# Grouped-query attention on one core: another order of the first query and key work, and a last unit whose final key chunk is closed apart

## The chip, the cores and the metric

The kernel runs on one NeuronCore of a Trainium2 chip. The core has five engines that work side by side, each through its own list of instructions in order: TensorE (PE) multiplies matrices, ScalarE (ACT) applies functions such as exp, VectorE (DVE) and GpSimd (POOL) do elementwise work, and SyncE (SP) issues transfers. ACT and POOL issue transfers too. Operands lie in the on-chip memory SBUF, and PE writes its results to PSUM, from where ACT and DVE read them. Engines wait for each other by semaphores.

The metric is the device time of one execution in microseconds (us). Less is better.

## The reference

```python
batch, seq, n_heads, n_kv_heads, dim = 8, 512, 32, 8, 64      # Q, K, V in float32
scale = 1.0 / np.sqrt(dim)
K_expanded = np.repeat(K, heads_per_group, axis=2)            # 4 query heads per key head
V_expanded = np.repeat(V, heads_per_group, axis=2)
scores = np.einsum('bhqd,bhkd->bhqk', Q, K_expanded) * scale  # after transposes to b, h, s, d
weights = np.exp(scores - np.max(scores, axis=-1, keepdims=True))
weights = weights / (np.sum(weights, axis=-1, keepdims=True) + 1e-10)
output = np.einsum('bhqk,bhkd->bhqd', weights, V_expanded)
return output.transpose(0, 2, 1, 3).astype(np.float32)
```

## The kernel before

**Units and tiles.** The work is cut into 32 units: 8 batches times 4 pairs of key heads. A unit has 8 query heads, two key heads, 512 queries and 512 keys. It is computed as 4 head pairs with 4 key chunks of 128 each, which makes 16 score tiles, numbered 0 to 15 within the unit (tile t belongs to head pair t // 4 and key chunk t % 4). `mm_scores` (L261) makes one tile: two matmuls with 64 contraction rows, one for each head of the pair, give 128 keys x (2 heads x 512 queries) in one of three PSUM slots. The scores come out transposed, keys on the partitions, so that the exponentials can be the weights of the next matmul.

**Exponentials.** A tile's exp is made by ACT (`exp_act`, L276, into tiles called `pa`) or by DVE (`exp_dve`, L285). The list `TILES` says which: 0 is ACT, 1 is DVE with one multiply and add whose result is read as bf16 bits (`pd`), 2 is DVE likewise (`lo`) followed by two additions on POOL (`hi`, L302, and `sum`, L308) that average two such approximations. Of 16 tiles, 11 are ACT's and 5 are DVE's; in all units the tile of kind 2 is tile 7. No maximum is subtracted.

**Outputs.** `mm_out` (L312) makes one output block: 128 queries of one head, four matmuls over the key chunks with the exponentials as weights, against the 64 value columns and a column of ones (65 in all, so that the sum of weights comes out beside the output). Blocks are grouped; a group fills one of two PSUM buffers called `x`, which the transposes use too. `take_out` (L328) copies a group to SBUF (`raw`), and after the unit's end `divide` (L352) takes the reciprocal on DVE (L355) and multiplies, on POOL (L360, two instructions of 128 x 1024 per unit), into `o_sb`, which `store` (L369) sends out by SP's queue. In the last unit the groups have 4 blocks (16 matmuls) each, eight groups in all; its first 16 blocks are multiplied by POOL, the next 8 by DVE (L360, 128 x 512), and the last two groups are multiplied by DVE straight from PSUM (128 x 256 each). The store of the very last group is issued on SP ahead of those of the unit's first 16 and next 8 blocks, that of the last but one on ACT's queue.

**Transposes.** Queries and keys are loaded with a cast to bf16 by POOL's queue (`load_q`, `load_k`, `load_v`; the first load of queries, `q_nat`, holds heads 4 to 7 of unit 0) and transposed on PE (`mm_turn`, L377), with a copy by DVE (`take_turn`, L389). Keys need a second copy with the two heads swapped, which two transfers on SP make (L395, L396). `spread_v` copies values beside the ones on POOL.

**The order.** Everything is recorded in an order planned ahead: the class `Plan` (L20) walks through the tiles with assumed costs, hands score tiles to ACT and DVE in the pattern `SCORES`, fills PE's time between them with transposes and output blocks, and returns one list of operations. The main loop (L494) records them in that order; nothing is moved afterwards, and each engine runs its list strictly in order. The planner's costs were not changed by the edit.

**The start.** Unit 0 does not wait for the casting loads. The first key pair (`k32`, 256 KB) and the first four query heads (`q32`, two halves of 256 KB) come in float32 by SP's and ACT's queues. DVE casts the keys (L468) and makes the swapped copy (L469, L470), ACT casts the first query half (L471). `turn_first` (L475) transposes, four transposes a time: keys, queries, swapped keys. Ten matmuls on zeros (L466) run on PE before that. The second query half is cast by DVE (L484) ahead of the main loop, and transposed in the main loop after the second score tile.

Of the kernel before, what the change touches and what calls it, by code (L numbers as in the profile page):

```python
# [11 lines left out]
BF16 = mybir.dt.bfloat16  # L12
# [8 lines left out]
NEVER = 1e9  # L21


class Plan:
# [14 lines left out]
    def __init__(self, nu, tiles, scores, fill, groups, arrive, x_cost, x_behind, fix, nslot, nx, npt):  # L39
        self.ops = []  # L40
        qa = [16 * u + t for u in range(nu) for t in range(16) if not tiles[t]]
        qd = [16 * u + t for u in range(nu) for t in range(16) if tiles[t]]
# [10 lines left out]
        def run_dve(until):  # L53
            nonlocal behind
            while ready:
# [9 lines left out]
                if j[1] == "score":  # L65
                    cost, vis = self.SCH, self.SCH_VIS
                    slots[j[3]] = start + vis
                    pt[j[2]] = start + vis + (fix if tiles[j[2] % 16] == 2 else 0.0)
# [102 lines left out]
def kernel(  # L171
# [24 lines left out]
    TILES = [int(c) for c in "0100010201000100"]  # L196
    SCORES = "AADAADAADAADAADA"
# [78 lines left out]
    def exp_act(t):  # L276
        pts[t] = pa_pool.tile([128, 2, S], BF16, name="pa")
        nc.scalar.activation(  # L278
            out=pts[t],
            in_=score.pop(t),  # L280
            func=mybir.ActivationFunctionType.Exp,
            scale=float(scale),
        )

    def exp_dve(t):  # L285
        two = TILES[t % len(TILES)] == 2
# [25 lines left out]
    def mm_out(f, at):  # L312
        _, u, lo, n = f
        if at == 0:
            xs[f] = xpsum.tile([128, 2048], U8, name="x").bitcast(FP32)
        i, r = divmod(lo + at, BLK)
        m, qc = divmod(r, SC)
        for kc in range(SC):
# [86 lines left out]

    turned = {}
# [26 lines left out]
    def arrive(f):  # L433
# [3 lines left out]
        NU, TILES, SCORES, FILL, groups, arrive, x_cost, x_behind,  # L437
# [3 lines left out]
    with tc.manual_schedule(engines={PE, ACT, DVE, POOL, SP}):  # L441
# [4 lines left out]
        k16 = first.tile([128, SC, 2, 2 * D], BF16, name="k16")  # L446
        warm = first.tile([128, S], BF16, name="warm")
        nc.sync.dma_start(out=k32, in_=rows(K, 0, 0, 2))
        nc.scalar.dma_start(out=q32[:, :, 0:2 * D], in_=rows(Q, 0, 0, 2))
        nc.sync.dma_start(out=q32[:, :, 2 * D:4 * D], in_=rows(Q, 0, 2, 4))  # L450
# [11 lines left out]
        load_q(1)  # L462

        xw = xpsum.tile([128, 2048], U8, name="x").bitcast(FP32)
        for _ in range(10):
            nc.tensor.matmul(xw, warm[:, 0:128], warm, start=True, stop=True)  # L466

        nc.vector.tensor_copy(out=k16[:, :, 0, :], in_=k32)  # L468
        nc.vector.tensor_copy(out=k16[:, :, 1, 0:D], in_=k32[:, :, D:2 * D])  # L469
        nc.vector.tensor_copy(out=k16[:, :, 1, D:2 * D], in_=k32[:, :, 0:D])  # L470
        nc.scalar.copy(out=q16[:, :, 0:2 * D], in_=q32[:, :, 0:2 * D])  # L471
# [3 lines left out]
        def turn_first(src, copy, dst):  # L475
            x = xpsum.tile([128, 2048], U8, name="x").bitcast(BF16)
            for sc in range(SC):
                nc.tensor.transpose(x[:, sc * 128:(sc + 1) * 128], src[:, sc, :], ident)  # L478
            copy(out=dst, in_=x[:, 0:S])  # L479
# [73 lines left out]
```

## Time and profile before

| | us |
|---|---|
| Median of 3 runs | 357.85 (357.47 to 357.93) |
| The profiled execution | 357.47 |
| Its span | 355.5 |
| Around the span | 1.97 |
| PE busy | 341.1 |
| DVE busy | 336.3 |
| ACT busy | 334.0 |
| POOL busy | 280.8 |
| First exp of ACT starts | 7.79 |
| Last exp of ACT starts | 343.92 |
| Last multiply of DVE starts | 349.46 |

All rows but the first two are of one profiled execution, in microseconds from the start of its span. Busy time counts an instruction from start to end, and instructions of one engine overlap at their ends: an exp is shown with 1.02 us, while the next one on ACT can start 0.90 after it. A row of a timeline gives start, duration, engine, source line, operation, output and input, and in brackets how long the engine was idle before and what released it. Rows of POOL are rough. A row of the table of stages gives, for a stretch, the busy time and number of instructions of PE, PE's weight loads, DVE, ACT and POOL, the clock that TensorE was granted (1.00 is full), the share of the transfer engines and GB/s.

### The profile page before, as it was taken

To read this page: it belongs to the slowest core of one execution; us is meant where nothing else is said; L and a number is where in the kernel's file an instruction comes from. 1 tells how busy PE (TensorE), PEld (TensorE's weight loads), DVE (VectorE), ACT (ScalarE), POOL (GpSimd) and SP (SyncE) were. 2 spreads that over 40 slices of the span, in tenths; PEclk is the share of its full clock that TensorE was granted. 3 is DMA by queue.
4 is the path that set the end of the run, shared out by engine and by line. 5 is a ranking of instruction groups with operands and counts; after the bars stand their busy time and mean duration, and the time that the engine had idled before them with its cause. 6 is when DMAs were issued, how large, how long until landed. Compare 5 with 4: busy or idle time off the path is not lost.

```text
span 355.5 us, 13278 instructions
## 1 busy us (share of the span) xinstructions
PE 341.1 (96%) x5774; PEld 223.9 (63%) x5774; DVE 336.3 (95%) x462; ACT 334.0 (94%) x355; POOL 280.8 (79%) x200
## 2 busy tenths in 40 slices
PE   7899999999999999999999999999999999999980
PEld 3366666666666666666666666666666666666660
DVE  3799999999999999999999999999999999999883
ACT  4999999999999999999999999999999999999960
POOL 6287977989778997789788897798977898866691
PEclk9899999999999999999999999999999999999997
DMA  8989765898778976699667987689757996722346
GB/s 181 207 146 193 194 162 157 190 208 204 171 181 190 258 191 143 128 236 240 164 182 168 205 209 193 157 189 246 192 129 181 202 251 177 190 75 79 120 164 194
DMA packets 51481, 64.42 MB, mean 181 GB/s; under 512 B 3424, under 2 KB 36064, under 8 KB 51424
## 3 DMA queue, kind: packets, MB, share of 16 engines
q0 software_dynamic: 25344, 24.91, 46.3%
q1 hardware_dynamic: 25024, 38.28, 31.7%
q8 instruction: 45, 0.74, 0.8%
q10 hardware_dynamic: 1056, 0.39, 0.4%
q14 instruction: 12, 0.10, 0.1%
HBM read 50.86 MB, written 33.55 MB: 237 GB/s over the span
## 4 chain that ended last, share of the span: by engine, by line
ACT 60%; issue 24%; PE 11%; DVE 3%; ACTq 0%; DVEq 0%
ACT pa L278 60%; PE x L319 4%; DVE pd L292 2%; PE x L466 1%; PE x L387 1%; DVE qt L401 0%; PE x L478 0%; DVE kt L479 0%; DVE raw L339 0%; PE s_256 L267 0%; PE s_237 L267 0%; ACTq L278 0%; DVE inv L355 0%; PE s_261 L267 0%; DVE o_sb L360 0%
## 5 line engine op out<-in xcount | busy, mean ns | idle before, releaser
L360 POOL TENSOR_TENSOR o_sb<-raw,inv 128x1024 f32<-128x1024 f32 x63 | 118.4, 1896 | 45.9 <-DVE inv L355 45.9
L319 PEld LDWEIGHTS <-pa 128*128 128x128 bf16 x2816 | 135.2, 98 | 29.4 <-issue 29.1
L319 PEld LDWEIGHTS <-pd 128*128 128x128 bf16 x1024 | 100.1, 98 | 0.6 <-issue 0.5
L267 PEld LDWEIGHTS <-kt 64*128 64x128 bf16 x1024 | 53.7, 94 | 71.6 <-issue 45.5
L339 DVE COPY raw<-x 128x455 f32<-128x455 f32 (+3 forms) x161 | 89.0, 570 | 0.7 <-PE x L319 0.5
L308 POOL TENSOR_TENSOR sum<-lo,hi 128x1024 bf16<-128x1024 bf16 x32 | 68.1, 2127 | 2.5
L302 POOL TENSOR_TENSOR hi<-lo,shift 128x512 int32<-128x512 int32 x32 | 40.8, 1275 | 9.3 <-DVE lo L292 9.2
L387 PE MATMUL x<-ident,q_nat 128*128 128x128 bf16 x504 | 44.3, 220 | 0.2 <-DMA q_nat<-in_Q_dram 0.2
L401 DVE COPY qt<-x 128x1024 bf16<-128x1024 bf16 x63 | 42.9, 681 | 0.0
L387 PEld LDWEIGHTS <-q_nat 128*128 128x128 bf16 x504 | 29.5, 97 | 16.0 <-issue 15.5
L237 POOL DMA_DIRECT2D q_nat<-in_Q_dram x32 | 25.6, 799 | 0.0
L319 PEld LDWEIGHTS <-sum 128*128 128x128 bf16 x256 | 24.8, 97 | 0.0
L319 PE MATMUL x<-v_5039,pa 128*128 128x65 bf16 x352 | 19.5, 194 | 0.0
L319 PE MATMUL x<-v_6090,pa 128*128 128x65 bf16 x352 | 19.4, 194 | 0.0
L319 PE MATMUL x<-v_2937,pa 128*128 128x65 bf16 x352 | 19.4, 194 | 0.0
L319 PE MATMUL x<-v_3988,pa 128*128 128x65 bf16 x352 | 19.4, 194 | 0.0
L319 PE MATMUL x<-v_835,pa 128*128 128x65 bf16 x352 | 19.4, 194 | 0.0
L319 PE MATMUL x<-v_1886,pa 128*128 128x65 bf16 x352 | 19.4, 194 | 0.0
L319 PE MATMUL x<-v_7141,pa 128*128 128x65 bf16 x352 | 19.0, 194 | 0.4 <-DVE raw L339 0.4
L319 PE MATMUL x<-v_5039,pd 128*128 128x65 bf16 x128 | 17.4, 194 | 0.0
L319 PE MATMUL x<-v_6090,pd 128*128 128x65 bf16 x128 | 17.3, 194 | 0.0
L319 PE MATMUL x<-v_2937,pd 128*128 128x65 bf16 x128 | 17.3, 194 | 0.0
(1091 smaller groups left out, 994.0 us busy)
## 6 DMA issues: line engine op xcount, KB each, us to landing
out_dram<-o_sb SPq DMA_DIRECT2D x30, 1024.0 KB, 4.8
q_nat<-in_Q_dram POOLq DMA_DIRECT2D x31, 512.0 KB, 5.9
k_nat<-in_K_dram POOLq DMA_DIRECT2D x8, 512.0 KB, 8.4
v_nat<-in_V_dram POOLq DMA_DIRECT2D x8, 512.0 KB, 11.0
kt<-kt SPq DMA_DIRECT2D x62, 64.0 KB, 5.3
out_dram<-o_sb SPq DMA_DIRECT2D x3, 512.0 KB, 3.6
q_105<-in_Q_dram ACTq DMA_DIRECT2D x1, 256.0 KB, 4.4
k_106<-in_K_dram SPq DMA_DIRECT2D x1, 256.0 KB, 3.9
```

Source lines behind the costliest of these rows:

```text
L237: nc.gpsimd.dma_start(out=t[:, :, lo * D:], in_=rows(Q, b, HU * gp + lo, HU * (gp + 1)))
L267: nc.tensor.matmul(s[:, m, :], kt[u][64 * m:64 * m + 64, 0 if m == g else 1, kc * 128:(kc + 1) * 128], qt[u][64 * m:64 * m + 64, i, :], st ...
L278: nc.scalar.activation(out=pts[t], in_=score.pop(t), func=mybir.ActivationFunctionType.Exp, scale=float(scale),)
L292: nc.vector.tensor_scalar(out=bits, in0=score.pop(t), scalar1=float(A_schr), scalar2=float(B_two if two else B_one), op0=mybir.AluOpType.mult,
L302: nc.gpsimd.tensor_tensor(out=high.rearrange("p m s -> p (m s)").bitcast(I32), in0=bits.rearrange("p m s -> p (m s)").bitcast(I32), in1=shift,
L308: nc.gpsimd.tensor_tensor(out=dst, in0=bits.bitcast(BF16), in1=high.bitcast(BF16), op=mybir.AluOpType.add)
L319: nc.tensor.matmul(xs[f][:, at * D1:(at + 1) * D1], pts[(u * HPG + i) * SC + kc][:, m, qc * 128:(qc + 1) * 128], v1[u][:, kc, 2 * i // HPG ...
L339: nc.vector.tensor_copy(out=raws[u][:, lo:lo + n, :], in_=x[:, 0:n * D1])
L360: eng.tensor_tensor(out=osbs[u].rearrange("p qc h d -> p h qc d")[:, lo // SC + h0:lo // SC + h0 + nh], in0=src[:, :, 0:D].rearrange("p (h ...
L387: nc.tensor.transpose(xs[f][:, at * 128:(at + 1) * 128], src, ident)
L401: nc.vector.tensor_copy(out=qt[u][:, 2 * part:2 * part + 2, :], in_=x)
L466: nc.tensor.matmul(xw, warm[:, 0:128], warm, start=True, stop=True)
```

## The change

The diff touches the first tiles and the last unit. Between them every engine has the same instructions in the same order.

*At the start.* The first key load is split: 128 keys (64 KB) first, the other 384 after the first query half has been issued. The first 128 keys are cast and swapped by DVE, transposed (both copies, two transposes) and copied in one go. The first query half is cast and copied by DVE instead of ACT. The other 384 keys are cast by ACT, swapped by POOL, transposed after the first score tile (six transposes) and copied by DVE in one instruction of 768 columns. The second query half is cast, transposed and copied after the fourth score tile: DVE's list has its cast behind DVE's first exp, where the cast was ahead of the main loop before. `load_v(0)` is issued ahead of POOL's swaps and of the cast of the first values, where it was behind that cast. There are 8 matmuls on zeros instead of 10.

*In the last unit.* The tile of kind 2 is tile 3 instead of 7. The exp of the very last tile is made in two halves, one per head. The last two output groups do their first three key chunks for all eight blocks, and then the fourth chunk for each group. The planner, which gets the tile kinds, puts the unit's last six score tiles ahead of all its output groups; before, the first head pair's outputs stood between them.

```diff
+    LAST_TILES = [int(c) for c in "0102010001000100"]
...
     def exp_act(t):
         pts[t] = pa_pool.tile([128, 2, S], BF16, name="pa")
+        dst, src = pts[t], score.pop(t)
+        for ms in (slice(0, 1), slice(1, 2)) if t == 16 * NU - 1 else (slice(0, 2),):
+            nc.scalar.activation(out=dst[:, ms, :], in_=src[:, ms, :],
...
-    def mm_out(f, at):
+    def mm_out(f, at, kcs=tuple(range(SC))):
         _, u, lo, n = f
-        if at == 0:
+        if at == 0 and kcs[0] == 0:
             xs[f] = xpsum.tile([128, 2048], U8, name="x").bitcast(FP32)
...
-        for kc in range(SC):
+        for kc in kcs:
...
+    def tile_kind(t):
+        return (LAST_TILES if t >= 16 * (NU - 1) else TILES)[t % 16]
...
-        nc.sync.dma_start(out=k32, in_=rows(K, 0, 0, 2))
+        nc.sync.dma_start(out=k32[:, 0:1], in_=rows(K, 0, 0, 2)[:, 0:1])
         nc.scalar.dma_start(out=q32[:, :, 0:2 * D], in_=rows(Q, 0, 0, 2))
+        nc.sync.dma_start(out=k32[:, 1:SC], in_=rows(K, 0, 0, 2)[:, 1:SC])
         nc.sync.dma_start(out=q32[:, :, 2 * D:4 * D], in_=rows(Q, 0, 2, 4))
         nc.sync.dma_start(out=v32, in_=rows(V, 0, 0, 2))
...
         load_q(0, lo=HPG)
         load_k(0)
         load_q(1)
+        load_v(0)
...
-        for _ in range(10):
+        for _ in range(8):
             nc.tensor.matmul(xw, warm[:, 0:128], warm, start=True, stop=True)
...
+        def cast_k(lo, hi, natural, swapped):
+            natural(out=k16[:, 0, lo:hi, :], in_=k32[:, lo:hi, :])
+            swapped(out=k16[:, 1, lo:hi, 0:D], in_=k32[:, lo:hi, D:2 * D])
+            swapped(out=k16[:, 1, lo:hi, D:2 * D], in_=k32[:, lo:hi, 0:D])
+
+        def turn_k(lo, hi):
+            x = xpsum.tile([128, 2048], U8, name="x").bitcast(BF16)
+            n = hi - lo
+            for c in range(2):
+                for sc in range(lo, hi):
+                    j = c * n + sc - lo
+                    nc.tensor.transpose(x[:, j * 128:(j + 1) * 128], k16[:, c, sc, :], ident)
+            nc.vector.tensor_copy(
+                out=kt[0][:, :, lo * 128:hi * 128],
+                in_=x[:, 0:2 * n * 128].rearrange("p (c s) -> p c s", c=2),
+            )
+
+        def turn_q(i):
+            lo, hi = 2 * i * D, 2 * (i + 1) * D
+            nc.vector.tensor_copy(out=q16[:, :, lo:hi], in_=q32[:, :, lo:hi])
+            x = xpsum.tile([128, 2048], U8, name="x").bitcast(BF16)
             for sc in range(SC):
+                nc.tensor.transpose(x[:, sc * 128:(sc + 1) * 128], q16[:, sc, lo:hi], ident)
+            nc.vector.tensor_copy(out=qt[0][:, i, :], in_=x[:, 0:S])
+
+        cast_k(0, 1, nc.vector.tensor_copy, nc.vector.tensor_copy)
+        turn_k(0, 1)
+        turn_q(0)
+        cast_k(1, SC, nc.scalar.copy, nc.gpsimd.tensor_copy)
         nc.gpsimd.tensor_copy(
             out=v1f[:, :, :, 0:D], in_=v32.rearrange("p sc (h d) -> p sc h d", h=2)
         )
-        load_v(0)
         load_q(2)
         load_q(3)
...
+        ends = [(NU - 1, 3 * BLK), (NU - 1, 3 * BLK + 4)]
...
+            elif kind == "out" and (what[0] if engine == "pe" else what)[1:3] in ends:
+                continue
...
+                if what[0] > 0 and scored < 100:
+                    turn_k(1, SC)
+                    scored = 100
                 mm_scores(*what)
+                scored += 1
+                if scored == 103:
+                    turn_q(1)
                     spread_v(0)
...
+        final = [("out", u, lo, 4) for u, lo in ends]
+        for kcs in (tuple(range(SC - 1)), (SC - 1,)):
+            for f in final:
+                for at in range(4):
+                    mm_out(f, at, kcs)
+                if kcs[-1] == SC - 1:
+                    take_out(f, NEVER)
```

## The prediction

> **What bounds the kernel now.** I read the page's busy shares first, then the table of stages, then the timelines of the first 24 and the last 15 us, because the diff leaves everything between them in the same order on every engine.
>
> ```profile
> span 355.5 us, 13278 instructions
> ...
> PE 341.1 (96%) x5774; PEld 223.9 (63%) x5774; DVE 336.3 (95%) x462; ACT 334.0 (94%) x355; POOL 280.8 (79%) x200
> ```
>
> ```profile
> 30.00:40.00 10.00, 9.95 (x175) 6.57 (x171) 9.99 (x14) 9.88 (x12) 8.26 (x7) 1.00 0.88 209
> ```
>
> The reader is to see that PE, DVE and ACT are all full between 20 and 330 us (the second fence is one row of the table of stages: busy time of PE, PEld, DVE, ACT and POOL in a stretch of 10). They feed each other in fixed orders. A stream that enters that stretch later leaves it later by as much; a saving counts only at the two ends.
>
> The start, from the timelines of DVE, ACT and PE (start, duration, engine, line):
>
> ```profile
> 6.88 0.43 DVE L479 COPY kt<-x 128x512 bf16<-128x512 bf16 x1 [0.47 <-PE x L478]
> 7.22 0.55 DVE L484 CAST q_108<-q_105 128x512 bf16<-128x512 f32 x1
> 8.33 0.42 DVE L479 COPY qt<-x 128x512 bf16<-128x512 bf16 x1 [0.57 <-PE x L478]
> 8.67 1.22 DVE L292 TENSOR_SCALAR pd<-s_191 128x1024 uint16<-128x1024 f32 x1
> 10.59 1.23 DVE L292 TENSOR_SCALAR pd<-s_213 128x1024 uint16<-128x1024 f32 x1 [0.70 <-PE s_213 L267]
> 11.73 0.68 DVE L401 COPY qt<-x 128x1024 bf16<-128x1024 bf16 x1
> ```
>
> ```profile
> 5.10 0.62 ACT L471 CAST q_108<-q_105 128x512 bf16<-128x512 f32 x1 [2.56 <-DMA q_105<-in_Q_dram]
> ...
> 7.79 1.02 ACT L278 ACTIVATE pa<-s_174 128x1024 bf16<-128x1024 f32 x1 [1.00 <-PE s_174 L267]
> ...
> 13.10 1.02 ACT L278 ACTIVATE pa<-s_237 128x1024 bf16<-128x1024 f32 x1
> ```
>
> ```profile
> 10.16 0.39 PE L267 MATMUL s_213<-qt,kt 64*128 64x512 bf16 x2
> ...
> 12.46 0.59 PE L267 MATMUL s_237<-qt,kt 64*128 64x512 bf16 x2 [0.32 <-DVE qt L401]
> ```
>
> The second half of the first queries is cast (7.22) and copied (8.33) before DVE's first exp, D1 (8.67). From there the path runs through D1, the second exp D5 (10.59), the next query copy (11.73) and the scores s_237 that wait for it. From 13.10 ACT has an exp every 0.90 to 1.09 us, hardly a gap.
>
> The end, from the timelines of DVE and POOL:
>
> ```profile
> 346.95 1.83 DVE L360 TENSOR_TENSOR o_sb<-raw,inv 128x512 f32<-128x512 f32 x1
> ...
> 349.46 0.42 DVE L360 TENSOR_TENSOR o_sb<-x,inv 128x256 f32<-128x256 f32 x1
> ```
>
> ```profile
> 339.17 1.28 POOL L302 TENSOR_TENSOR hi<-lo,shift 128x512 int32<-128x512 int32 x1 [0.31 <-DVE lo L292]
> ...
> 342.60 5.63 POOL L360 TENSOR_TENSOR o_sb<-raw,inv 128x1024 f32<-128x1024 f32 x3
> ```
>
> DVE's multiply of 512 elements takes 1.83 where one of 256 takes 0.42, and it ends (348.78) 0.55 after POOL's third multiply (342.60 + 5.63 = 348.23). I read it as held up by POOL: POOL's last multiply, not DVE's queue, sets the last stores.
>
> **The change part by part: the start.** Steps are start-to-start from the rows above and their neighbours.
>
> *First chunk.* A key DMA of 64 KB goes ahead, the other 192 KB follow as a further SP issue (0.42 to 0.50), in front of the second query half and v32 (wanted at 9.87 and by POOL at about 6.9: hidden). Three small DVE casts, two transposes and a copy replace 0.43 + 0.29 + 0.29 of casts. They cost nothing if done by 5.10, when the queries land: true if the chunk lands by about 4. It lands after 2.4 (the DMA table shows hardly a byte before) and by 4.64 (the whole key load now). Nearest is a 128 KB store with 2.1 us from issue to landing; I take 3.4, cost 0. Two warm-up matmuls fewer (0.43 each) free PE at 4.6.
>
> *First queries.* Cast and copy go from ACT to DVE: cast 5.10, transposes 5.78 (0.68, as 7.22 to 7.90), copy 6.21 (0.43), scores 6.70 (0.49, as 6.88 to 7.37), first exp 7.12 instead of 7.79: 0.67 early.
>
> *Rest of the keys.* ACT casts 384 columns (0.62 x 384/512 = 0.47) from about 4.7. POOL makes two swaps of 192 (0.61 for 512 in its v1f cast: about 0.25 each). load_v(0) is now in front of them (issue 0.75 from 4.16): 4.9 to 5.4. Six transposes follow the first scores: 6.92 to 7.43. One DVE copy of 768, between 0.42 (512) and 0.68 (1024): 0.55, so scores at 8.07 and 8.29, and D1 at 8.29 + 0.44 = 8.73, against 8.67: nothing gained. In between ACT idles; the third exp stays at 9.68, behind the q_nat transposes, which wait for their DMA until 8.80. The v1f cast, now behind load_v(0) and the swaps, waits for v32 until 6.88 as before.
>
> POOL's swaps may hold the query cast: 0.55 beside POOL's v1f cast against 0.43 for the same size alone gives 0.12 at most by rows, less than nothing is excluded, and I leave it in the range. [...]
>
> *Second queries.* This is the costly move. Their cast is now behind D1 in DVE's queue, their transposes behind the fourth scores on PE. D1 8.73, cast 9.87 (1.14, as 10.59 to 11.73), transposes 10.55, copy 10.98, scores of ACT's fourth tile 11.47, of DVE's second 11.69 (0.22 apart), D5 12.12 (0.43): against 10.59, **1.53 late**. Behind D5 wait the next query copy 13.26, the scores that read it 13.99 and their exp 14.63 against 13.10. From there to 18.74 six exps take 5.64 where 0.92 each would be 5.5, so about 0.13 is caught up: **+1.40**.
>
> *load_v(0)* is issued 3.3 earlier but behind the same two loads in its queue; its reader waits until 16.46, as the queue serves about 2.5 us per load (8.80, 11.31). The loads q2 and q3 keep their order. Cost 0.
>
> **The end.** The two-octave tile moves from 7 to 3, so its lo comes at 335.79 and POOL's hi no longer waits 0.31: hi 338.87, sum to 342.35. The first output group needs it at 343.0, which is the cover. All six last scores now precede the unit's eight output groups: last scores at 342.67 (now 343.18), groups of 16 matmuls at 0.03 = 0.48 each, two PSUM buffers, each freed 0.47 after its copy starts. The copies of the third, fourth, fifth and sixth group start at 344.86, 345.34, 346.04, 346.48; now the last of them is at 346.18 (chain of waits), so DVE is 0.30 late. POOL's third multiply needs the reciprocal after the fourth copy: 346.1, after its own second (342.3 + 2 x 1.88 = 346.06), so it ends at 348.0 instead of 348.23, and DVE's held multiply with it: **-0.25**. Bounds: -0.3 (the idle removed) and +0.4 (DVE's side sets the end, and slips by 0.1 more). I take -0.25, as the 1.83 shows who waits for whom. The halved last exp (one instruction more) ends at about 344.5 and the split groups need it at 347.3: cost 0, and gain 0. The final stores keep their order.
>
> **Sum.** +1.40 - 0.25 = +1.15. The profiled execution took 357.47 (span 355.5 and 1.97 around it), so 358.6; it is the fastest of three, the median is 357.85, so I predict 359.0.
>
> **Rivals.**
> *The clock falls sooner.* The table of stages:
>
> ```profile
> 12.50:15.90 3.40, 3.14 (x14) 0.92 (x13) 1.78 (x3) 3.35 (x4) 0.00 (x0) 0.50 1.25 207
> ```
>
> The granted clock is 0.50 there, after a sparse stretch, and score pairs take 0.6 instead of 0.39. The new order is sparser from 5.7 on. If it falls at 9.1, two pairs cost +0.45 and four transposes +0.2, and s_237 saves 0.2: 359.45. Against: it held at 1.00 through 11 to 12.5. [...]
> *The chunk is not early.* Landing at 4.64, casts, transposes and copy (1.78 now, from 4.64 to 6.42, for four times the columns; I take 1.25) push the query cast to about 5.9: +0.8, 359.8.
> *Absorbed.* The first query half lands with less in front of it, by at most 0.9 (0.55 MB have moved by 4.2): D5 at 11.22, +0.63 - 0.13 - 0.25 = +0.25, 358.1.
> *Faster.* The lead of 0.67 at the first exp is carried through: 357.85 - 0.67 - 0.25 = 356.9. It needs D5 at 9.9, so the queries landed before 2.9; break-even, with D5 at 10.6, is at about 3.6. Against: 256 KB in front of 5.10 are not less now, and q_nat at 8.80 bars PE.
>
> **How the numbers follow.** Forecast 0.49, clock 0.14, chunk 0.10, absorbed 0.17, faster 0.10. A measurement tells about 0.2%, 0.72 us, from no change. The first three are slower, less a margin of the forecast: 0.71; absorbed and that margin are within: 0.18; faster 0.11. The range goes from 358.0 (absorbed, with the tail's best bound) to 360.2 (clock or chunk with the POOL hold or the tail's +0.4); the forecast's own is 358.4 to 359.6.
>
> **What would show it.** First exp at about 7.1; third still 9.7; D1 at 8.7 with the query cast behind it; fourth exp at about 11.9 against 10.60, with over 1 us of ACT idle; D5 near 12.1; from 20 us every row late by about 1.4. At the end the last POOL multiply 0.25 earlier, counted from ACT's exp of the last unit's tile 10 (338.95 now), and DVE's still held. I am wrong if D5 starts by 11, if the unit period after 20 us (10.46) shrinks, or if DVE's last multiply takes 0.6.

## The result: 361.8 us, slower by 1.2%, and the profile after

The changed kernel takes 361.81 us (median of 4 runs, 361.13 to 362.33), the kernel before beside it 357.66. The ratio is 1.0119, with a 95% interval of 1.0091 to 1.0148. The profiled execution took 362.32, with a span of 360.3; all numbers of the profile below are of this one execution, against the profiled one of before (357.47). The direction was forecast, the size was not: 359.0 was predicted, with a range up to 360.2, and 361.8 lies beyond it.

The first page lines of the kernel after, and its row of the table of stages for 30 to 40 us:

```profile
span 360.3 us, 13278 instructions
...
PE 343.8 (95%) x5772; PEld 224.6 (62%) x5772; DVE 336.6 (93%) x464; ACT 333.8 (93%) x355; POOL 281.6 (78%) x202
```

```profile
30.00:40.00 10.00, 9.95 (x171) 6.46 (x168) 9.90 (x15) 9.88 (x12) 7.45 (x5) 1.00 0.85 145
```

The engines do the same work, and the middle is nearly as full as it was. DVE and ACT are busy for as long as before (336.6 and 333.8 us against 336.3 and 334.0), so for them the 4.8 us that the span is longer are idle time. To see where they enter, I compared the start of each of ACT's exps with the same exp of the kernel before (the numbers in the last line of the block are after minus before):

```
ACT's exp         1st    2nd    3rd    4th    6th   10th   13th   31st   41st  105th  169th  235th  301st
kernel before    7.79   8.71   9.68  10.60  13.10  16.93  19.64  36.71    ...
late by         -0.32  +0.79  +1.54  +2.71  +3.16  +3.74  +3.76  +3.74  +3.93  +4.18  +4.48  +4.78  +4.97
```

So 3.75 us are lost before 20 us, and 1.25 more in five steps of 0.21 to 0.29, each at one exp: the 38th, 102nd, 166th, 230th and 294th, always 64 exps apart. From the 348th exp, that of the last unit's tile 10, the shift is 4.99. The last multiply of DVE is late by 4.87, and what follows it is 0.08 shorter: 4.8 in all.

**The start.** DVE, ACT and PE in the kernel after (start, duration, engine, line):

```profile
5.23 0.42 DVE L498 CAST q_108<-q_105 128x512 bf16<-128x512 f32 x1
...
9.92 1.23 DVE L295 TENSOR_SCALAR pd<-s_183 128x1024 uint16<-128x1024 f32 x1 [1.14 <-PE s_183 L268]
11.06 0.42 DVE L498 CAST q_108<-q_105 128x512 bf16<-128x512 f32 x1
12.18 0.42 DVE L502 COPY qt<-x 128x512 bf16<-128x512 bf16 x1 [0.70 <-PE x L501]
13.73 1.22 DVE L295 TENSOR_SCALAR pd<-s_215 128x1024 uint16<-128x1024 f32 x1 [1.13 <-PE s_215 L268]
```

```profile
7.47 1.02 ACT L281 ACTIVATE pa<-s_167 128x1024 bf16<-128x1024 f32 x1 [1.98 <-PE s_167 L268]
...
16.25 1.02 ACT L281 ACTIVATE pa<-s_239 128x1024 bf16<-128x1024 f32 x1 [0.30 <-PE s_239 L268]
```

```profile
5.71 0.61 PE L501 MATMUL x<-ident,q_108 128*128 128x128 bf16 x4 [0.72 <-DVE q_108 L498]
6.83 0.61 PE L268 MATMUL s_167<-qt,kt 64*128 64x512 bf16 x2 [0.51 <-DVE qt L502]
```

The order is the forecast one: D1 (9.92), the cast behind it, copy, D5 (13.73). But every link with PE in it is longer. Four transposes take 0.61 and a score pair 0.61, where the kernel before shows 0.40 and 0.39 at full clock (the transposes of before, then a score pair of after behind 20.7):

```profile
7.90 0.40 PE L478 MATMUL x<-ident,q_108 128*128 128x128 bf16 x4
```

```profile
21.82 0.39 PE L268 MATMUL s_313<-qt,kt 64*128 64x512 bf16 x2
```

The long ones go on until 20.7:

```profile
13.88:17.29 3.41, 2.69 (x14) 0.95 (x12) 2.62 (x4) 2.51 (x4) 0.00 (x0) 1.00 1.24 206
17.29:20.70 3.41, 3.37 (x19) 1.49 (x20) 2.52 (x3) 2.87 (x4) 3.05 (x2) 1.00 1.20 212
20.70:24.12 3.42, 3.35 (x52) 1.96 (x49) 3.14 (x5) 3.42 (x4) 3.34 (x4) 1.00 0.32 58
```

These are rows of the table of stages. Here the column of the granted clock misleads: it prints 1.00 in all three. The trace's own clock records begin with the first grant, at 20.71, and what lies ahead of the first record is printed as full. The durations say half: from 20.71 on a score pair takes 0.39 again. In the kernel before the first grant is at 5.70. Where the grants fall is not the same in each execution: of the other three of the kernel after, two (361.30 and 361.13) have a mean granted clock of 0.978 and 0.982 against 0.993 here, which fits a grant that came early and was lost again, as in run 1 below; no trace of them shows it.

**The five steps.** ACT of the kernel after around one of them, and PE's row for the scores in question:

```profile
107.43 1.02 ACT L281 ACTIVATE pa<-s_2416 128x1024 bf16<-128x1024 f32 x1
108.62 1.02 ACT L281 ACTIVATE pa<-s_2467 128x1024 bf16<-128x1024 f32 x1 [0.17 <-PE s_2470 L268]
```

```profile
107.85 0.39 PE L268 MATMUL s_2467<-qt,kt 64*128 64x512 bf16 x2
```

The exp of s_2467 starts 0.38 after its scores are done (108.24). The profile puts the wait down to s_2470, which this exp does not read: a releaser is inferred, and here it is the wrong one. The engine waited for nothing that the profile shows.

**The end.** DVE and POOL:

```profile
352.37 1.29 DVE L363 TENSOR_TENSOR o_sb<-raw,inv 128x512 f32<-128x512 f32 x1
...
354.33 0.42 DVE L363 TENSOR_TENSOR o_sb<-x,inv 128x256 f32<-128x256 f32 x1
```

```profile
343.81 1.27 POOL L305 TENSOR_TENSOR hi<-lo,shift 128x512 int32<-128x512 int32 x1
...
351.21 1.90 POOL L363 TENSOR_TENSOR o_sb<-raw,inv 128x1024 f32<-128x1024 f32 x1 [0.21 <-DVE inv L358]
```

POOL's hi waits for nothing any more, but its last multiply waits 0.21 for DVE's reciprocal. Counted from the shift of 4.99, POOL's last multiply starts at 346.22 (346.33 before), DVE's multiply ends at 348.67 (348.78 before), and the end gains 0.12. In all 18 profiles of this case DVE's multiply ends 0.54 to 0.55 behind POOL's last one, whether it is shown with 1.3 or with 1.8.

### The profile page after: what moved, and what is told of

The parts are those of the page before. It is cut to its first block, busy times and chain, and to the rows that moved or that the text cites. A ratio compares the mean times of both kernels' runs of the same rounds, so it can differ in the third digit from the quotient of the medians.

```text
span 360.3 us, 13278 instructions
## 1 busy us (share of the span) xinstructions
PE 343.8 (95%) x5772; PEld 224.6 (62%) x5772; DVE 336.6 (93%) x464; ACT 333.8 (93%) x355; POOL 281.6 (78%) x202
## 4 chain that ended last, share of the span: by engine, by line
ACT 59%; issue 23%; PE 14%; DVE 3%; ACTq 0%; DVEq 0%
ACT pa L281 59%; PE x L322 5%; PE x L390 1%; DVE pd L295 1%; PE x L474 1%; PE x L501 0%; PE x L490 0%; DVE o_sb L363 0%; DVE raw L342 0%; DVE qt L502 0%; DVE kt L491 0%; DVE q_108 L498 0%; PE s_239 L268 0%; PE s_258 L268 0%; PE s_210 L268 0%
## 5 line engine op out<-in xcount | busy, mean ns | idle before, releaser
L390 PE MATMUL x<-ident,q_nat 128*128 128x128 bf16 x504 | 45.2, 223 | 0.0
```

What stands on the lines that cost most here:

```text
L390: nc.tensor.transpose(xs[f][:, at * 128:(at + 1) * 128], src, ident)
```

## Experiments

Three theories were tested: the new *order* costs 1.4 to 1.5 as forecast; the *clock*, half until 20.7, costs the rest of the start; the *place in ACT's list* makes the five steps. "Late" below is the start of ACT's exp against the same exp in the kernel before, in the profiled execution; the time before is that measured on the same chip. Where an expectation speaks of the exp of the 13th tile, ACT's 13th exp is meant.

**1. One more ACT instruction in the kernel after.**

```diff
+        pad = first.tile([128, 1], BF16, name="pad")
+        nc.scalar.copy(out=pad, in_=warm[:, 0:1])
         cast_k(0, 1, nc.vector.tensor_copy, nc.vector.tensor_copy)
```

> The changed kernel with one more ACT instruction (a copy of one column) ahead of its key cast, nothing else. Why: against the kernel before, ACT's 38th, 102nd, 166th, 230th and 294th exp of the changed kernel each start 0.2 to 0.27 us late, 64 exps apart, with their scores long done; the change took one instruction out of ACT's list, so that something that recurs along that list now meets an exp instead of the event instruction ahead of it. Theory 'place in ACT's list': the five delays vanish, 5 x 0.25 = 1.2 us, so 361.8 becomes about 360.6, with the first 24 us as they are. Rival 'the delays come from the order of the work or from the transfers': one instruction at the start changes nothing, 361.8, and the five delays stay.

360.08 against 357.45, ratio 1.0069 (1.0044 to 1.0095). All five steps are gone: 2.81 late at the 13th exp, 2.76 at the 301st. (The clock was full from 5.43 to 8.84 here and half until 19.08, which fits 2.8 and not 3.75 at the start.) Nothing else separates it from the kernel after behind 20 us but the list and, as run 15 shows, 32 bytes of address.

**2. Ten matmuls on zeros again.**

```diff
-        for _ in range(8):
+        for _ in range(10):
```

> The changed kernel with 10 matmuls on zeros instead of 8. In the changed kernel a score pair takes 0.61 us, not 0.39, from the first until 20 us, so TensorE runs at half clock there; before, that was so only from 12.5 to 15.9. Theory 'clock lost with the two matmuls': pairs of 0.39 from about 6 us on. The first transposes of keys now stand behind the zeros until 5.6, so the first exp comes at about 8.2, but the later steps are short: the exp of the tenth tile comes about 2.5 late against the kernel before instead of 3.75, so about 360.6. Rival 'the clock is lost for another reason' (thin work later on): pairs stay at 0.61, and the first transposes come 0.7 later, so about 362.5.

362.91, ratio 1.0130 (1.0092 to 1.0169). The full clock is there from 5.39, is lost at 8.80 and comes back only at 22.46; the 13th exp is 4.54 late. The two zeros alone are not what was missing: TensorE was busy 1.53 of 3.41 us after the grant, and the grant did not last. (This run has one more step, of 0.29 at the 248th exp, and run 9 one of 0.22 at the same one. No costly entry stands there, and no run says why.)

**3. Four zeros in the gaps of the kernel after**, two behind `turn_k(0, 1)`, one behind `turn_q(0)`, one ahead of `turn_k(1, SC)`:

```diff
+            for _ in range(n):
+                nc.tensor.matmul(s[:, 0, :], warm[:, 0:128], warm, start=True, stop=True)
```

> The changed kernel, where four matmuls on zeros (512 columns, 0.43 us each at half clock) fill PE's waits: two behind the first key transposes, one behind the first query transposes, one behind the six later key transposes; their results are not read. Theory 'clock': with PE kept busy from 1.2 to about 6 it gets its full clock as before, pairs take 0.39, and the start loses what was worked out from the order alone, 1.4 to 1.9, instead of 3.75: about 359.7 to 360.2. Rival 'order alone': the loss of 3.75 stays with pairs at 0.39 or not, 361.8 or some tenths more.

361.06, ratio 1.0088 (1.0069 to 1.0107). Full clock from 7.04 to 13.87, half until 20.69, which fits a time above the one expected. While it was full, the chain reaches D5 within a tenth of the forecast:

```profile
12.22 1.23 DVE L295 TENSOR_SCALAR pd<-s 128x1024 uint16<-128x1024 f32 x1 [0.70 <-PE s L268]
```

D5 was forecast for 12.12. (D1 stands at 9.05, 0.32 later than forecast; the steps behind it are shorter than worked out.) The sixth exp is 1.65 late (1.53 forecast), and 2.70 at the 13th, behind the half clock.

**4. The second query half earlier**, after the second score tile:

```diff
-                if scored == 103:
+                if scored == 101:
```

> The changed kernel with the second query half's cast, transposes and copy after the second score tile (as in the kernel before) instead of the fourth: DVE's cast and copy stand ahead of its first exp again. Clock untouched, so half clock is expected here too. Theory 'second queries behind the first DVE exp': from DVE's first to its second exp 3.81 us fall to about 1.9, DVE's first exp comes about 0.4 later, so 1.5 less: about 360.3. Rival 'the clock alone': the order does not matter once each step is slow, 361.8.

360.98, ratio 1.0084 (1.0058 to 1.0111). Cast and copy are ahead of D1 again, D5 follows D1 by 2.35 instead of 3.81, and the sixth exp is 2.31 late: 0.85 of the 1.5 come back, with the clock at half until 12.94 and again from 16.36.

**5. One more ACT instruction in the kernel before**: the two lines of run 1, ahead of its query cast.

> The kernel before, with one ScalarE copy of one column ahead of its query cast, so that every later instruction of ScalarE's list moves on by one copy and its exps land on the places that they have in the kernel after. Theory (place in the list): what costs the kernel after five times 0.21 to 0.29 us is an exp that sits on a certain place of ScalarE's list, and has nothing to do with the new order at the start. Then the 37th, 101st, 165th, 229th and 293rd exps here each start 0.2 to 0.3 us later against the kernel before than the exp ahead of them did; the last exp is 1.2 late, and the time about 358.9 (358.5 to 359.2). Rival (the steps belong to the late start of the kernel after): no step anywhere, every exp within 0.1 of the kernel before, 357.6.

357.01 against 357.40, ratio 0.9979 (0.9968 to 0.9989), and no step. The theory fell in this form, and ACT's list of recorded entries, counted from 0, says why (an entry is an instruction or a wait for a semaphore, and each exp has such a wait ahead of it; the times are those from this wait's start to the exp's, at the five places):

```
                                exp of the scores just made        0.06 to 0.16 is usual
kernel after   entries 63, 191, 319, 447, 575     0.37 0.34 0.35 0.34 0.34
kernel before  entries 64, 192, 320, 448, 576     0.16 0.06 0.06 0.06 0.06
run 1          entries 64, 192, 320, 448, 576     0.17 0.06 0.06 0.06 0.06
run 5          entries 65, 193, 321, 449, 577     0.16 0.06 0.06 0.06 0.06
```

So it may be an exp on entry 63, or 128 entries on, that costs. In run 5 that entry is the exp ahead of these, which stands behind a running exp anyway (0.34 to 0.77), and the wait would be hidden. Run 6 tests it.

**6. One ACT instruction fewer in the kernel before**, so that the same exps stand on entries 63, 191 and so on:

```diff
-        nc.scalar.dma_start(out=q32[:, :, 0:2 * D], in_=rows(Q, 0, 0, 2))
+        nc.sync.dma_start(out=q32[:, :, 0:2 * D], in_=rows(Q, 0, 0, 2))
```

> The kernel before, with its first query load issued by the queue of SP in place of ScalarE's, so that ScalarE's list is one entry shorter and its exps stand at the places that they have in the kernel after (the 37th recorded exp on recorded entry 63, the next ones 128 entries apart). The copy put ahead in the kernel before moved them the other way and cost nothing. Theory (the wait lies ahead of recorded entry 63 and every 128th behind it; it shows only where that entry is an exp whose scores come late, as in the kernel after, and is hidden where ScalarE still works on the exp ahead, as in the kernel before and with the copy): five steps of 0.2 to 0.3 at the 38th, 102nd, 166th, 230th and 294th exp, each with about 0.34 between the wait entry and the exp in place of 0.06, together 1.1 to 1.4 us behind whatever the later query load costs at the start (0 to 0.5): 358.4 to 359.4. Rival (the five steps belong to something else of the kernel after): no steps, 357.2 to 358.0.

361.01 against 358.01, ratio 1.0104 (1.0061 to 1.0148). The five steps are there, 0.21, 0.28, 0.28, 0.28 and 0.30, with 0.34 to 0.37 between wait and exp:

```profile
105.77 1.02 ACT L278 ACTIVATE pa<-s 128x1024 bf16<-128x1024 f32 x1
106.95 1.02 ACT L278 ACTIVATE pa<-s 128x1024 bf16<-128x1024 f32 x1 [0.17 <-PE s L267]
```

That settles the place in the list. The later query load cost more than I allowed, 2.08 at 25 us; run 9 tells why.

**7. The kernel before without zeros**, its whole `for _ in range(10)` loop left out:

> The kernel before without its ten matmuls on zeros: the old order, with the clock at half from the start until TensorE's own work is granted the full one. It prices the half clock by itself. Theory (half clock through the start costs about as much as the kernel after lost by it): no full clock in the records before 12 us, transposes of four at 0.6 us and score pairs at 0.6, VectorE's second exp 1.2 to 2.5 later than 10.59, the exps from 25 us on 1.0 to 2.5 later, 358.5 to 360.0. Rival (the price of the forecast, 0.45 net, since exps and not TensorE set the start): the exps from 25 us on 0.2 to 0.7 later, 357.6 to 358.2.

358.88, ratio 1.0027 (1.0012 to 1.0041). First grant at 13.06, D5 at 12.01 (1.42 late), the exps from 25 us on 1.08 late. PE in the stretch at half clock:

```profile
5.95 0.61 PE L474 MATMUL x<-ident,q 128*128 128x128 bf16 x4
6.35 0.63 PE L474 MATMUL x<-ident,k 128*128 128x128 bf16 x4
```

By itself, in the old order, half clock until 13.06, some 7 us more of it at this place, cost 1.1, not 0.45. (The kernel before has its half clock from 12.53 to 15.94; here it is full from 13.06 on.)

**8. Zeros behind every score pair of the kernel before**, tiles 2 to 12:

```diff
                 mm_scores(*what)
+                if 2 <= what[0] <= 12:
+                    keep_busy(1)          # one matmul on zeros into an x buffer
```

> The kernel before, with one matmul on zeros (0.22 us at full clock, nobody reads it) behind each score pair of tiles 2 to 12, so that TensorE has no idle stretch there. Theory (the clock follows TensorE's busy time in stretches of 3.41 us): in the records so far full clock was kept after stretches with 2.31 us and more of busy time and lost after 2.24 and less, and granted after 2.98 and more, not after 2.92 and less. The kernel before loses it at 12.5 us after a stretch with 2.24 and has it back at 15.9. With the zeros every stretch from 6 to 20 us has over 2.6, the records show no half clock between its first grant and 20 us, and the exps from the ninth tile on come 0.1 to 0.6 earlier: 357.0 to 357.5. Rival (ScalarE is busy 3.36 of the 3.41 us of half clock, so that the slow TensorE is hidden there): the half clock goes but no exp from 20 us on moves by more than 0.1, 357.6. Rival (the zeros stand ahead of score pairs that somebody waits for): the exps come 0.2 to 0.8 later, up to 358.4.

358.68, ratio 1.0029 (1.0019 to 1.0040). The clock never fell, and the exps from 20 us on are 1.45 late. The second rival holds, beyond its own price (up to 358.4): the zeros need a buffer, and wait for its reader:

```profile
13.22 0.38 PE L445 MATMUL x<-warm 128*128 128x512 bf16 x1 [0.89 <-DVE qt L404]
```

The same zeros in the kernel after, with the edits of runs 1 and 4, for tiles 1 to 14 (**run 10**):

> The kernel after with all three causes taken away at once: the ScalarE copy of one column that moves its exps off the costly places, the second query half turned after the second score tile and not after the fourth, and matmuls on zeros (two behind the first key chunk, one behind the first query half, one behind each score pair of tiles 1 to 14) that keep TensorE busy. Theory (order, clock and list place together are the whole loss): no steps of 0.2 in the exps, VectorE's second exp within 0.5 of the 10.59 of before and not at 13.73, the clock full from 7 us on at the latest, the exp of the 13th tile 0 to 0.6 later than before, and with 0.12 gained at the end 357.6 to 358.2. Rival (something else of the new start costs, the late chunks of the key or GpSimd's casts): the exp of the 13th tile is 1.0 to 2.0 late with full clock all along, 358.7 to 359.7. Rival (the zeros hold up the score pairs): the late exps show pairs that wait behind a zeros matmul, and 358.5 to 359.5.

359.57, ratio 1.0046 (1.0031 to 1.0061); full clock from 5.83, no steps, the 13th exp 2.93 late. As in run 8 the zeros are in the way (the one at 13.71 waits 0.89 for DVE's copy), so it does not tell the causes apart.

**9. The end of the change alone**, on the start of the kernel before:

> The end of the change alone: the start of the kernel before, with the tiles of the last unit dealt anew, the last exp in two halves, and the last two output groups closed chunk by chunk. The forecast had 0.25 us less for this; the kernel after showed 0.12 less behind its own shift. Theory (the last multiply of VectorE sets the end, and starts when the last sums of its group are closed): the exps up to the last unit stand as in the kernel before, VectorE's last multiply ends 0.1 to 0.15 earlier than 349.46 + its own length, the time 357.3 to 357.6, not to be told from before by the times alone, but by the trace. Rival (the forecast): 0.25 earlier, with GpSimd's third multiply at 348.0. Rival (the second visit to the two groups costs TensorE as much as it saves): within 0.05.

357.32 against 357.40, ratio 0.9998 (0.9982 to 1.0013). Counted from its exps (+0.09), the last multiply is 0.12 early. But this run and run 5 show something else. At 18 us their exps stand at -0.47 and -0.08; at 25 us and later at -0.13 and +0.27. POOL's copy of V (the spread) in run 9, in run 5 and in the kernel before:

```profile
16.33 1.89 POOL L256 COPY v<-v_nat 128x2048 bf16<-128x2048 bf16 x1 [6.42 <-DMA v_nat<-in_V_dram]
```

```profile
16.73 1.89 POOL L255 COPY v<-v_nat 128x2048 bf16<-128x2048 bf16 x1 [6.78 <-DMA v_nat<-in_V_dram]
```

```profile
16.46 1.90 POOL L255 COPY v_186<-v_nat 128x2048 bf16<-128x2048 bf16 x1 [6.54 <-DMA v_nat<-in_V_dram]
```

The copies of runs 9 and 5 start at -0.13 and +0.27 against before, exactly the shift of all that follows. In run 6 it starts at 18.55 (+2.09), and the exps are 2.08 late. In POOL's list the first `hi` and `sum` stand behind the copy, so the later of the two, the landing of V or the first exps, sets the start. In the kernel before they lie close together: in run 15 the copy starts at 15.78 (-0.68), the exps stand at -0.10 at 18 us, and from 25 us on only 0.07 is gained.

**11. The V spread behind the first sum**, on run 9's kernel:

```diff
                 exp_dve(what)
+                if what == TILES.index(2):
+                    spread_v(0)
```

> The start of the kernel before with the end of the change, and one more edit: GpSimd's spread of the first V batch stands behind the first half-octave sum and not ahead of it. In the kernel before and in the two runs made from it the spread began when the V batch had landed (16.46, 16.73, 16.33 us), the sum behind it ended 5.3 later, and the shift of every exp from 25 us on was that of the spread (0, +0.27, -0.13), whatever the exps at 18 us had gained (0, -0.08, -0.47). Theory (the landing of V, by way of GpSimd's list, sets the start of the kernel before): now the sum is done by 18 us, the exps from 25 us on stand 0.3 to 0.6 earlier than in the kernel before, and the time is 356.8 to 357.2, below both kernels. Rival (the next limit lies right behind it, or the spread is then late for the second unit): within 0.1 of the run with the end alone, 357.3.

357.46 against 358.01, ratio 0.9984 (0.9970 to 0.9997). The profiled execution, at 358.59 the slowest of ten, lost the clock from 11.45 to 18.27 and was 1.04 late, so the trace did not decide; run 14 does.

**12. The V load of the kernel after put back** behind the cast of the first V half:

> The kernel after with its load of the first V batch put back behind GpSimd's cast of the first V half, where the kernel before has it. In the kernel after that cast waited 5.68 us for its own data, to 11.54, and the spread began at 17.65 in place of 16.46. Theory (the start of the kernel after is set by order and clock, which are later than V either way): the cast runs by 8 us, the spread begins at 16.3 to 17.0, and the exps from 25 us on stand within 0.3 of the kernel after, as far as the clock records are alike; 361.0 to 362.2. Rival (the early V load takes the transfers' share from the key chunks and the second query half and is what makes the start late): the exps from 25 us on 0.8 to 2 earlier, 359.5 to 360.8.

362.47, ratio 1.0130 (1.0112 to 1.0147). First grant at 19.77, the exps from 25 us on 3.63 late, against 3.73 in the kernel after: the moved load is no cause. This run shows something else beside it. DVE's first query cast and POOL's second key swap, of run 12 and then of the kernel after:

```profile
5.24 0.61 DVE L497 CAST q<-q 128x512 bf16<-128x512 f32 x1
5.23 0.34 POOL L481 CAST k<-k 128x192 bf16<-128x192 f32 x1
```

```profile
5.23 0.42 DVE L498 CAST q_108<-q_105 128x512 bf16<-128x512 f32 x1
5.30 0.55 POOL L482 CAST k_109<-k_106 128x192 bf16<-128x192 f32 x1
```

The one that starts first takes the shorter time (0.34 in run 12, 0.42 in the kernel after), and the other is about 0.2 longer (0.61, 0.55). Runs 1 and 4 agree with run 12 (swap first, cast 0.59), runs 3 and 13 with the kernel after (cast first, 0.42).

**13. The new order at full clock.** Run 1's copy, run 3's zeros, and nine more where PE waits for DVE anyway (six by `PRE`, ahead of a pair in its own buffer, and three ahead of the second query half's transposes, not shown):

```diff
+    PRE = {4: 2, 8: 3, 12: 1}
...
+        for _ in range(PRE.get(t, 0)):
+            nc.tensor.matmul(s[:, 0, :], warm[:, 0:128], warm, start=True, stop=True)
```

> The kernel after with the ScalarE copy of one column, and with matmuls on zeros only where TensorE waits for something else anyway: two behind the first key chunk, one behind the first query half, one ahead of the other key chunks, three while it waits for the cast of the second query half and two while it waits for that half's copy, three ahead of the score pair of the eighth tile and one ahead of the twelfth's. Theory (the new order costs 1.4 to 1.5 at full clock, and all the rest of the start is the half clock): full clock from 7 to 20 us in the records, VectorE's second exp at 12.0 to 12.4, the exp of the 13th tile and the exps from 25 us on 1.3 to 1.7 late, no steps; 358.6 to 359.3. Rival (something besides order, clock and list place): full clock in the records, and the exps from 25 us on 2.2 to 2.9 late, 359.5 to 360.4. Where the records show half clock in spite of the zeros the run tells nothing of either.

358.59 against 357.65, ratio 1.0024 (1.0013 to 1.0035). Full clock from 6.42 on, no steps:

```profile
8.97 1.23 DVE L299 TENSOR_SCALAR pd<-s 128x1024 uint16<-128x1024 f32 x1 [0.70 <-PE s L272]
10.11 0.42 DVE L501 CAST q<-q 128x512 bf16<-128x512 f32 x1
11.02 0.42 DVE L508 COPY qt<-x 128x512 bf16<-128x512 bf16 x1 [0.49 <-PE x L507]
12.14 1.23 DVE L299 TENSOR_SCALAR pd<-s 128x1024 uint16<-128x1024 f32 x1 [0.70 <-PE s L272]
```

```profile
11.49 0.61 PE L272 MATMUL s<-qt,kt 64*128 64x512 bf16 x4
```

Two score pairs now take the 0.61 that one took. The exps are 1.31 late at the 13th and 1.33 from 25 us on. The copy of V starts at 17.31, only 0.85 late, so V's landing is not what makes the 1.33. So the order costs 1.33, and of the 3.75 of the kernel after the other 2.4 are the clock, by subtraction.

**14. Run 11 with six zeros** where PE waits for transfers:

```diff
+            for _ in range({(0, 1): 2, (1, None): 4}.get((u, part), 0)):
+                nc.tensor.matmul(x.bitcast(FP32), warm[:, 0:128], warm, start=True, stop=True)
```

> The start of the kernel before, the end of the change, the V spread behind the first half-octave sum, and six matmuls on zeros where TensorE waits for transfers: two ahead of the first transposes of the casted query half, four ahead of those of the key. Theory (V's landing by way of GpSimd's list, and now and then the clock, set the start of the kernel before): no half clock between the first grant and 20 us, the exps from 25 us on 0.3 to 0.6 earlier than in the kernel before, 356.6 to 357.1, below both kernels. Rival (the next limit lies right behind V's landing): clock full, and the exps from 25 us on within 0.2 of the kernel before, 357.2 to 357.6. Rival (zeros in the way): the first score pairs later than 7.9, 357.6 or more.

357.10 against 357.65, ratio 0.9985 (0.9976 to 0.9994). The clock stays full, the sum is done before V is spread, and the exps from 25 us on are 0.38 early:

```profile
15.53 2.12 POOL L312 TENSOR_TENSOR sum<-lo,hi 128x1024 bf16<-128x1024 bf16 x1
17.60 0.24 POOL L256 MEMSET v<- 128x32 bf16 x1
17.66 1.89 POOL L257 COPY v<-v_nat 128x2048 bf16<-128x2048 bf16 x1
```

**15 and 16. Thirty-two bytes.** Run 5 was faster than the kernel before although its exps were 0.2 late. In the runs with the copy (1, 5, 10, 13) 5.11 to 5.21 us lie between DVE's last multiply and the end of the span, in all others 5.52 to 5.63. The copy's tile moves every pool behind it by 32 bytes, the output tiles `o_sb` from address 189408 to 189440 on each partition. A tile that nothing touches does the same, in the kernel before (15) and in run 14's kernel (16):

```diff
+        gap = first.tile([128, 1], BF16, name="gap")
```

> The kernel before, with a tile of one column in the pool of the first tiles that no instruction touches. It moves the pools behind it, the output tiles o_sb among them, by 32 bytes, from 189408 to 189440 on each partition. Theory (stores from an address that is a multiple of 64 move faster): 5.1 to 5.25 us between the end of VectorE's last multiply and the end of the span in place of 5.62, and 356.8 to 357.3. Rival (ScalarE's list, not the place in SBUF, shortened the end): 5.5 to 5.65, and no difference, 357.4 to 357.8.

> The kernel with the old start, the new end, the later V spread and six zeros where TensorE waits for transfers (357.10 measured), with the same untouched tile. Theory (the two gains are independent, 0.38 at the exps and 0.4 behind the last multiply): end part 5.1 to 5.25, 356.5 to 356.9, ratio to the kernel before 0.996 to 0.998. Rival (ScalarE's list): no change against 357.1.

Run 15: 357.16 against 357.52, ratio 0.9993 (0.9984 to 1.0002), end part 5.18. Run 16: 356.67, ratio 0.9978 (0.9969 to 0.9987), end part 5.20, exps 0.64 early (0.26 more than in run 14, and no run says why). The times of run 15 alone do not tell it from before; the end part does, in six of six kernels. The transfers issued in the last 11 us (KB, median us from issue to landing), the kernel before and then run 15:

```profile
out_dram<-o_sb SPq DMA_DIRECT2D x3, 512.0 KB, 3.6
out_dram<-o_sb SPq DMA_DIRECT2D x1, 256.0 KB, 3.5
```

```profile
out_dram<-o_sb SPq DMA_DIRECT2D x3, 512.0 KB, 3.0
out_dram<-o_sb SPq DMA_DIRECT2D x1, 256.0 KB, 3.1
```

Run 16 is the fastest kernel here, 0.2% below the one before and 1.4% below the one after (356.67 to 361.81, the two not timed on the same chip). It has the end of the change, not its start, and on top of that the later V spread, six zeros and the untouched tile.

## Why the prediction was wrong, step by step

The late multiply of 4.87 in the profiled execution, by the runs: order 1.33 (run 13), half clock 2.4 (3.75 less 1.33), list 1.25 (five steps, runs 1 and 6), end -0.12.

- **Second queries, +1.40: right.** D5 at 12.14 and 12.22 against 12.12, and 1.33 from 25 us on, once the clock is full. That D5 fits so closely is in part luck: in run 13 D1 is 0.24 later than forecast (8.97, not 8.73), and the copy follows the cast by 0.91, not 1.11. *First chunk* cost nothing, as said (landing by 3.32, forecast 3.4). The hold of the query cast by POOL's swaps, left in the range with 0.12 at most by rows, is there in some runs, with 0.2 (0.61 for 0.42, run 12), but not in the profiled execution.
- **V: two waits were wrong, and cost nothing here (run 12).** The v1f cast was to wait for v32 until 6.88 as before; it waited until 11.54. The V spread was to start at 16.46 as before; it starts at 17.65. Both are hidden behind the exps, which are 3.75 late. At full clock too the spread stays 0.85 late (run 13), a limit that would be left if the order cost nothing.
- **The clock: the rival was named, and mis-sized; this is the term that failed first.** The forecast's own sum put it at nothing, because the clock of the kernel before held through 11 to 12.5. As a rival it had a chance of 0.14 and a price of +0.45, for two pairs and four transposes behind one loss at 9.1. In truth the new order left TensorE with 2.17, 2.77, 2.53 and 2.69 us of work in the four stretches of 3.41 from 3.64 to 17.29, without a grant, and 3.37 in the one that ends with it; with zeros in its gaps (run 13) the clock was full from 6.42 on. At half clock four transposes and a score pair took 0.61 each in place of 0.40 and 0.39, in every link of the chain that has PE in it. The half clock lasted until 20.7 and cost 2.4 in this execution. "Two warm-up matmuls fewer" was costed by the time that they free, not by what they bring to the clock; run 2 shows that they alone would not have saved it.
- **"From 20 us every row late by about 1.4": failed, and no rival had it.** *First queries* costed the move of a cast and a copy from ACT to DVE on DVE only. It also took one entry out of ACT's list, and five exps came to stand on entries that cost 0.2 to 0.3 each, 1.25 together. In the middle, where all engines are full, none of it came back: the shift grows from 3.74 at the 31st exp to 4.97 at the 301st.
- **The end, -0.25: half of it.** The mechanism held: DVE's multiply still ends 0.55 behind POOL's third. But that one starts at 346.22, not 346.1, because the reciprocal is later than worked out.
- **"Faster" had a limit in its way that it did not name.** It carried a lead of 0.67 through. In the kernel before the spread of V is a limit right behind the first exps: run 9's lead of 0.47 shrank to 0.13, and in the kernel after the spread starts later still.
- Absorbed and the late chunk did not occur.

The clock records of the runs show this much: between two records in the first 25 us all stretches last 3.41, 6.83, 10.24 or more such steps (the kernel before from 5.70 to 12.53 and on to 15.94, run 1 from 5.43 to 8.84 and on to 19.08). A full grant came after stretches of 3.41 with 2.98 us or more of busy TensorE (2.98 in run 1), yet not after 3.03 and 3.16 in two runs (11 and 7); it was lost after 1.53 (run 2) to 2.23 (the kernel before), and kept after 2.13 (run 7) and more. No threshold was shown.

## What to carry to other kernels

Where the start can run at half clock, as TensorE did here until 20.7 us (a score pair in 0.61, not 0.39), cost a sparser order at both clocks, to the end of the sparse stretch, and put filler only where TensorE waits anyway: in its own buffer, never ahead of something that is awaited (a zero of run 8 waited 0.89 for its buffer, and the exps came 1.45 late). Compare instruction counts per engine as well as order: one entry more or less moves every later entry, and its sign here was a shift of all exps in like steps (0.21 to 0.29), at equal distances (64 exps). And before a start is made faster, look for the next limit behind it: the first rows whose shift does not follow the first exps.

## What was not expected of the hardware

- An exp on recorded entry 63 of ACT's list, and on each of the four entries at steps of 128 behind it, started 0.34 to 0.38 after the wait ahead of it, not 0.06 to 0.16. All six kernels in which these exps read scores just made show it (the kernel after and runs 2, 3, 4, 6 and 12); in run 5, where such an entry is an exp that stands behind a running one (0.34 to 0.77), no step is seen. Why was not shown. The profile of the kernel after lists 12 packets of 8 KB on a queue named instruction, and none of them moves just ahead of the five exps: the next one starts 0.7 to 3.3 behind each, the last one ahead of it 1.5 or more before.
- The granted clock printed ahead of the first record (20.71 in the kernel after) is 1.00 while four transposes take 0.61: durations decide.
- A DVE cast and a POOL cast that meet, both from SBUF to SBUF (the first query cast and the second key swap): the second to start took about 0.2 longer (DVE 0.61 for 0.42 in run 12, POOL 0.55 for 0.34 in the kernel after).
- Output tiles 32 bytes further on (189440 for 189408) shorten the end by 0.41 to 0.44 (runs 16 and 15); three of the last transfers land after a median of 3.0 us in run 15, against 3.6 in the kernel before. No run tried other addresses, so the multiple of 64 of run 15's expectation was not shown.
